# A differential-attention encoder on one core: the heads' norm factors sent through DRAM instead of through TensorE, and a branch's splits spread over four merge tiles

## The chip, the core and the metric

The kernel runs on one core of a Trainium2 chip. A core has TensorE (PE; its weight loads are listed as PEld), VectorE (DVE), ScalarE (ACT), GpSimd (POOL), and SyncE (SP), whose queue issues nearly all DMAs of this kernel. On-chip tensors lie on 128 partitions; TensorE writes to accumulation banks of 128 x 512 floats, of which there are eight. The time is that of the device in microseconds (us); the profile is of one further execution of the same program.

## The reference, cut to what matters

Two sequences of 512 tokens go through one encoder layer. Three branches (a state-space branch, a differential attention, an attention to a memory) are computed from the normed input, each is projected up, gated and added, and an output projection and a gated feed-forward layer follow. The change lies in the differential attention's norm and in the merge of the branches:

```python
def _diff_attention(q, k, v, lam, subln_g, lambda_init):
    ...
        w = probs[:, :, 0] - lam * probs[:, :, 1]
        return jnp.einsum('bhqk,bkhe->bqhe', w.astype(v.dtype), v)
    ...
    o = _rmsnorm(o, subln_g) * (1.0 - lambda_init)
    return o.reshape(Bn, L, DIFF_WIDTH)

def _layer(x, mem, l, p):
    ...
    branches = (y_s5, y_diff, y_x)
    merged = None
    for n in range(N_BRANCH):
        term = jax.nn.sigmoid(g[..., n * D_MODEL:(n + 1) * D_MODEL]) * (branches[n] @ p['w_up'][l, n])
        merged = term if merged is None else merged + term
    x = x + merged @ p['w_out'][l]
```

There are 4 differential heads of width 128, `D_MODEL` is 1024 and a branch is 512 wide. The norm is over the 128 features of one head, one factor for each token.

## The kernel before

Activations lie transposed: features on partitions, tokens along the free dimension. A float32 product is made of three products of rounded parts: each operand is split into a high and a low part (`split`: ScalarE makes the high part, VectorE the low one), and `mm3` adds high x high, high x low and low x high into one bank, 512 columns at a time. A weight tile is loaded to `wf` (two buffers), split to `wh` and `wl` (two buffers each), and used.

The stage of the change is the differential attention. Its 32 steps run over 4 heads, 2 sequences and 4 blocks of 128 queries (`steps`, (h, s, qt)). Step i goes through the loop at the end in stages, one turn of the loop apart:

- `score` makes two maps' scores in banks of the pool `sc` (three banks) and the softmax parts on VectorE and ScalarE: `nb` is the negated maximum, `e` the exponentials, later the weighted difference of both maps, `r` the reciprocal sums.
- `turn` transposes `e` on TensorE (bank `bktr`, two banks) and splits it to `pH` and `pL`.
- `outputs` multiplies with the values for each pair of blocks, into the one bank `oo`; after the fourth block ScalarE copies it to `osb` (features x tokens).
- `squares`, after the fourth block, transposes `osb`, sums squares on ScalarE into `ss` (tokens on partitions), and adds the softmax's part of epsilon.
- `normed`, one turn later, makes the factors and scales. `factor` first calls `root`: a square root on ScalarE and a reciprocal on VectorE, `rs`, 128 x 4: one factor for each token, tokens on partitions. To scale `osb`, whose tokens lie along the free dimension, the factors have to stand on all partitions along that dimension; `spread` does this by four transposes of a broadcast column each into a bank. VectorE scales `osb` from that bank, and SP stores it to `bD[1, h]` in DRAM.

All of this is laid between other products. `queue` is a list of generators (projections of the next heads, gates, the merges), and `fill(10)`, called twice in each turn, takes about ten products from it. TensorE's order is the program's order from here on (`PE.on`). The order on the other engines and on SP's queue is set by a scheduler when the program is built: an instruction may stand well ahead of its place in the code.

The last generator is `merges`. For the output tiles m = 0 to 7 it multiplies the first branch (n = 0) with `w_up[0, m]` into two banks of the pool `mm`, which has two banks in all; VectorE takes each out with its gate, `mg <- gl, bkmm`. Then the third branch (n = 2) follows in the same way, `gl <- gl, bkmm`, with a sum on GpSimd. A branch comes back from DRAM by `merge_part`: a load of 128 x 1024 from `bD[n, t]` into `yt` (one of the four buffers `ld`, which gates and gate loads use too) and a split to `yh` and `yl`. Before the change `merge_in(2)` makes all four parts of the third branch at tile m = 5 of the first. After the attention loop the second branch (n = 1, the differential one) is split between the last products of the queue and merged last.

`mbc` is a tile of 128 x 512 that an earlier stage uses for the memory's norm factors and nobody after that.

Of the kernel before, what the change touches and what calls it, by code (L numbers as in the profile page):

```python
# [10 lines left out]
F32 = mybir.dt.float32  # L11
# [3 lines left out]
ALU = mybir.AluOpType  # L15
# [4 lines left out]
P = 128  # L20
L = 512
DM = 1024
KD = DM // P
NS = 2
# [46 lines left out]
def encoder(ctx: ExitStack, tc: tile.TileContext, a, out, out_t):  # L71
    nc = tc.nc
    V, S, PO, PE, SP = (InOrder(tc, e_) for e_ in (nc.vector, nc.scalar, nc.gpsimd, nc.tensor, nc.sync))
# [17 lines left out]
    def open_tags(es, side=None, **tags):  # L91

        for tag, n in tags.items():
            pools[tag] = es.enter_context(tc.tile_pool(name=tag, bufs=n, side=side, reuse_waits="tile"))
# [12 lines left out]
    drp = ctx.enter_context(tc.tile_pool(name="drp", bufs=1, space=DRAM))  # L107

    def slot(tag, shape=(P, NT), dt=F32, name="sl"):
        return pools[tag].tile(list(shape), dt, tag=tag, name=name)  # L110
# [21 lines left out]
    def split(hi, lo, src, scale=None):  # L132

        if scale is None:
            h = S.copy(hi, src)
            l_ = V.tensor_tensor(out=lo, in0=src, in1=hi.bitcast(F32), op=ALU.subtract)
        else:
            h = S.activation(out=hi, in_=src, func=AF.Copy, scale=scale)
            l_ = V.scalar_tensor_tensor(out=lo, in0=src, scalar=scale, in1=hi.bitcast(F32), op0=ALU.mult, op1=ALU.subtract)
        return h, l_  # L140
# [64 lines left out]
    def root(ss, n, nt=4, bias=epsc):  # L205

        rs = rp.tile([P, 4], F32, tag="rs", name="rs", bufs=4)
        S.activation(out=rs[:, :nt], in_=ss[:, :nt], func=AF.Sqrt, scale=1.0 / n, bias=bias)
        V.reciprocal(rs[:, :nt], rs[:, :nt])
        return rs  # L210

    def factor(ss, n, nt=4, bias=epsc):
        rs = root(ss, n, nt, bias)
        return rs, spread(rs, nt)

    def spread(rs, nt=4):

        bc = aux()
        for t in range(nt):
            PE.transpose(bc[:, t * P : (t + 1) * P], rs[:, t : t + 1].broadcast_to([P, P]), ident)  # L220
        return bc
# [24 lines left out]
    def sums(src, tag="wb", ss=None, ts=range(4)):  # L246

        if ss is None:
            ss = rp.tile([P, 4], F32, tag="ss", name="ss", bufs=3)
        for t in ts:  # L250
            tk = slot(tag, [P, DM], name="tk")
            SP.dma_start(tk, src[t])
            S.activation(out=tk, in_=tk, func=AF.Square, accum_out=ss[:, t : t + 1])
        return ss
# [107 lines left out]
    bc = spread(rs)  # L362
# [26 lines left out]
    bc = spread(rs)  # L389
# [102 lines left out]
    g04 = cst.tile([P, 1], F32, name="g04")  # L492
# [81 lines left out]
    with behind():  # L574

        mrs = cst.tile([P, 4], F32, name="mrs")
        mbc = cst.tile([P, L], F32, name="mbc")
        rs_, bc = factor(sums(a["memN"], "ld"), DM)
# [65 lines left out]
    def fill(n):  # L644
        nonlocal owed
        owed += n
        while owed > 0 and queue:
            r = next(queue[0], None)
            if r is None:
                queue.pop(0)  # L650
            else:
                owed -= r
        if not queue:
            owed = 0
# [5 lines left out]
    def units(src, hi, lo, use, nk=KD):  # L660

        wh, wl = weight(src, nk * P)
        for s in range(NS):
            cs = slice(s * L, (s + 1) * L)
            o = bank()
            for k in range(nk):
                mm3([o], wh, wl, [(hi[k][:, cs], lo[k][:, cs])], k, nk)
                if k == nk - 1:
                    use(s, o)
                if k % 2 == 1:  # L670
                    yield 6

    def gate_units():
        t = next(todo)
        gt = slot("ld", name="gt")

        def use(s, o):
            S.activation(out=gt[:, s * L : (s + 1) * L], in_=o, func=AF.Tanh, scale=0.5)

        yield from units(a["w_in"][20 + t], xh, xl, use)  # L680
        SP.dma_start(gD[t], gt)
# [43 lines left out]
    steps = [(h, s, lt) for h in range(4) for s in range(NS) for lt in range(4)]  # L725
# [3 lines left out]
    for i in range(-AHEAD, len(steps) + 1):  # L729
        if i + AHEAD < len(steps):  # L730
            h, s, lt = steps[i + AHEAD]
# [18 lines left out]
        if 0 <= i < len(steps):  # L750
            h, s, lt = steps[i]
# [8 lines left out]
        if i > 0 and steps[i - 1][2] == 3:  # L760
            h, s, _ = steps[i - 1]
# [7 lines left out]
            osb = xa.tile([P, L], F32, tag="osb", name="xosb", bufs=1)  # L769
# [57 lines left out]
    def merge_part(n, t, tag="y"):  # L827
        h_, l_ = (slot(tag, [P, NT], F32R, f"y{c}{t}") for c in "hl")
        yt = slot("ld", name="yt")
        SP.dma_start(yt, bD[n, t])  # L830
        split(h_, l_, yt, scale=(0.125, None, 0.5)[n])
        return h_, l_

    def merge_in(n, tags="yyyy"):
        return list(zip(*(merge_part(n, t, tags[t]) for t in range(4))))

    def merge_units(n, b, m, first=False, last=False):
        gt = slot("ld", name="gl")
        SP.dma_start(gt, gD[n * KD + m])
        if first:  # L840
            mg[m] = slot("mg", name=f"mg{m}")

        def use(s, o):
            cs = slice(s * L, (s + 1) * L)
            dst = mg[m] if first else gt
            V.scalar_tensor_tensor(out=dst[:, cs], in0=gt[:, cs], scalar=1.0, in1=o, op0=ALU.add, op1=ALU.mult)

        yield from units(a["w_up"][n, m], *b, use, 4)
        if not first:
            PO.tensor_tensor(out=mg[m], in0=mg[m], in1=gt, op=ALU.add)  # L850
        if last:
            mgh[m] = slot("ms", [P, NT], F32R, f"mgh{m}")
            mgl[m] = slot("ms", [P, NT], F32R, f"mgl{m}")
            split(mgh[m], mgl[m], mg[m])
# [4 lines left out]
    def first_in(t):  # L859
        parts0[t] = merge_part(0, t, ("qk", "qk", "qk", "v")[t])  # L860
        if len(parts0) == 4:
            b0.append(list(zip(*(parts0[t_] for t_ in range(4)))))

    def merges():
        res_.close()
        xp_es.close()
        open_tags(mes, side="right", mg=8, y=8)
        for m in range(KD):
            if m == 5:
                b2 = merge_in(2)  # L870
            yield from merge_units(0, b0[0], m, first=True)
        for m in range(KD):
            yield from merge_units(2, b2, m)

# [7 lines left out]
    for _ in gate_units():  # L882
# [3 lines left out]
    queue += [qk_units(1, True), dk[1], gate_units(), qk_units(2, True), dk[2], v1_, qk_units(3, True), dk[3], gate_units(),  # L886
              gate_units(), merges()]
    s0, ss, osb = {}, {}, {}

    def score(i):  # L890
        nonlocal last_e
        h, s, qt = steps[i]
        cs = slice(s * L, (s + 1) * L)
        if h and s == qt == 0:
            finish(dk[h])
        if qt == 0:
            s0[h, s] = acol.tile([P, 4], F32, tag="s0", name="s0", bufs=3)
        q_, k_, er = qk[h, True], qk[h, False], []
        qs_ = slice(s * L + qt * P, s * L + (qt + 1) * P)
        sc = [bank("sc") for _ in MAPS]  # L900
        for mp in range(2):
            PE.matmul(sc[mp], q_[mp][:, qs_], k_[mp][:, cs], start=True, stop=False)
            PE.matmul(sc[mp], q_[mp][:, qs_], k_[2 + mp][:, cs], start=False, stop=True)
        for mp in range(2):
            er.append(softmax_parts(ap_, acol, sc[mp], L, 1.0, f"d{mp}", None if mp else s0[h, s][:, qt : qt + 1]))
        (e0, sm0), (e1, r1) = er
        V.scalar_tensor_tensor(out=r1, in0=r1, scalar=nlam, in1=sm0, op0=ALU.mult, op1=ALU.mult)
        last_e = last_x, V.scalar_tensor_tensor(out=e0, in0=e1, scalar=r1, in1=e0, op0=ALU.mult, op1=ALU.add)
        es[i] = e0
# [32 lines left out]
    def squares(i):  # L942
# [9 lines left out]
        V.scalar_tensor_tensor(out=s0[h, s], in0=s0[h, s], scalar=EPS * P, in1=s0[h, s], op0=ALU.mult, op1=ALU.mult)  # L952
        V.tensor_tensor(out=ss[h, s], in0=ss[h, s], in1=s0[h, s], op=ALU.add)

    def normed(i):
        h, s, _ = steps[i]
        _, bc = factor(ss[h, s], P, bias=0.0)
        V.scalar_tensor_tensor(out=osb[h, s], in0=osb[h, s], scalar=g04, in1=bc, op0=ALU.mult, op1=ALU.mult)
        SP.dma_start(bD[1, h, :, s * L : (s + 1) * L], osb[h, s])

    n = len(steps)
    for i in range(-1, n + 3):
        if i + 1 < n:
            score(i + 1)
        if i in (22, 23):
            first_in(2 * i - 44)
        fill(10)
        if i in (21, 22):
            first_in(3 if i == 21 else 1)
        if 0 <= i < n:  # L970
            turn(i)
        if 0 < i <= n and steps[i - 1][2] % 2:
            outputs(i - 1)
        fill(10)
        if 1 < i <= n + 1 and steps[i - 2][2] == 3:
            squares(i - 2)
        if i > 2 and steps[i - 3][2] == 3:
            normed(i - 3)
    aes.close()
    phase.close()  # L980
    ves.close()
# [334 lines left out]
    for i in range(1, KFF - 1):  # L1316
        n = i + 1
# [209 lines left out]
    for v, (m, lo_, hi_) in enumerate(VISITS):  # L1527
# [24 lines left out]
        if v == 0:  # L1552
# [3 lines left out]
            y = [y2[m // 2][:, m % 2] for m in range(KD)]  # L1556
# [40 lines left out]
    for i, (c0, n) in enumerate(parts):  # L1597
        before, acc = acc if i else None, new_acc()
        for m in range(KD):
# [7 lines left out]
            if i and m == 3:  # L1607
                bc = spread(rs)
# [30 lines left out]
    bc = spread(rs, 3)  # L1639
# [461 lines left out]
```

## Time and profile before

| | us |
|---|---|
| three runs: median (lowest to highest) | 1585.29 (1582.87 to 1586.84) |
| the profiled execution, its own time | 1587.09 |
| its span, from the first instruction to the last | 1584.2 |
| differential attention with the merges laid into it | about 535 to 762 |
| first to last transposes of norm factors there | 572.7 to 759.6 |
| stores of scaled heads, `bD<-osb`, first to last issue | 574.1 to 760.9 |

In the lists a row of a timeline is start, duration, engine, line, operation, written tile <- read tiles, shapes, and in brackets how long the engine stood idle before it and who released it. All compute instructions pass through one helper and carry its line, L62, so that tiles tell them apart. A list of DMAs gives the number of issues, the size of one and the median time from issue to landing. A list by stage gives busy time of each engine, the granted TensorE clock, the share of time in which the DMA engines were busy, and GB/s.

### The profile page before, as it was taken

What the parts mean: (1) busy time and instruction counts of PE and PEld (TensorE: products, weight loads), DVE (VectorE), ACT (ScalarE), POOL (GpSimd) and SP (SyncE); (2) the same over time, 40 slices, a digit from 0 to 9 for tenths busy, and PEclk for the clock granted to TensorE, in tenths of its full rate; (3) what the DMA queues carried; (4) which work ended last, traced back from release to release, by engine and by line L of the source; (5) the groups of instructions that cost most, each with busy time, mean ns of one, the idle gap of its engine ahead of it and who ended that gap; (6) DMA issues with size and microseconds to landing.
All of it is one profiled execution on the core that took longest, in us unless ns stands there. A gap on an engine that the chain in (4) does not pass through costs nothing.

```text
span 1584.2 us, 21534 instructions
## 1 busy us (share of the span) xinstructions
PE 1573.7 (99%) x7701; PEld 1320.9 (83%) x7701; DVE 1119.0 (71%) x1777; ACT 627.2 (40%) x1112; POOL 510.5 (32%) x406
## 2 busy tenths in 40 slices
PE   9999999999999999999999999999999999999998
PEld 7888888888898889888888888888888888878887
DVE  5897688665766676866445567777767777999664
ACT  7354322346553356564223353232333223333222
POOL 0001000001432221300343335767655542445353
PEclk9999999999999999999999999999999999999999
DMA  9643362567655543354544433555433241786632
GB/s 350 208 144 142 102 222 80 184 192 257 205 180 163 149 117 84 110 186 167 175 156 154 153 100 126 179 183 182 160 126 133 107 153 69 272 279 202 212 120 106
DMA packets 118970, 261.04 MB, mean 165 GB/s; under 512 B 15824, under 2 KB 51920, under 8 KB 118864
## 3 DMA queue, kind: packets, MB, share of 16 engines
q1 hardware_dynamic: 117856, 256.80, 48.6%
q10 hardware_dynamic: 1008, 2.88, 0.5%
q8 instruction: 60, 0.98, 0.2%
q14 instruction: 46, 0.38, 0.1%
HBM read 172.89 MB, written 74.15 MB: 156 GB/s over the span
## 4 chain that ended last, share of the span: by engine, by line
PE 94%; DVE 2%; DMA 2%; ACT 1%; issue 1%; SPq 0%; DVEq 0%; ACTq 0%
PE bkmm L62 81%; PE bktr L62 8%; PE bksc L62 3%; PE bkoo L62 2%; DVE tl L62 1%; DMA tk<-in_memN 1%; DMA acc<-in_w_fo 0%; DMA wf<-in_w_mv 0%; DVE ts L62 0%; DVE y L62 0%; ACT tk L62 0%; DVE u L62 0%; ACT th L62 0%; DVE w L62 0%; ACT L62 0%
## 5 line engine op out<-in xcount | busy, mean ns | idle before, releaser
L62 PE MATMUL bkmm<-xh,wh 128*128 128x512 f32 x640 | 252.7, 395 | 0.0
L62 PE MATMUL bkmm<-xl,wh 128*128 128x512 f32 x640 | 250.7, 392 | 0.0
L62 PE MATMUL bkmm<-xh,wl 128*128 128x512 f32 x640 | 249.8, 391 | 0.0
L62 PE MATMUL bkmm<-th,whl 128*128 128x512 f32 x696 | 227.3, 390 | 0.0
L62 ACT CAST wh<-wf 128x1024 fp32r<-128x1024 f32 (+1 forms) x131 | 116.1, 886 | 228.1 <-PE bkmm L62 189.2
L62 DVE TENSOR_TENSOR wl<-wf,wh 128x1024 fp32r<-128x1024 f32 (+1 forms) x132 | 141.5, 1072 | 69.3 <-ACT wh L62 66.0
L62 PEld LDWEIGHTS bkmm<-th,whl 128*128 128x128 f32 x696 | 130.6, 188 | 27.2 <-issue 0.2
L62 PEld LDWEIGHTS bkmm<-xh,wl 128*128 128x128 f32 x640 | 120.2, 188 | 25.5 <-issue 0.2
L62 PE MATMUL bkmm<-th,w 128*128 128x512 f32 x432 | 140.4, 391 | 0.9 <-DVE up L62 0.5
L62 POOL TENSOR_TENSOR raw<-raw 128x128 f32<-128x128 f32 x144 | 90.5, 629 | 155.7 <-DMA raw<-in_w_fo 128.9
L62 PEld LDWEIGHTS bkmm<-xh,wh 128*128 128x128 f32 x640 | 120.3, 188 | 23.3 <-issue 0.2
L62 PEld LDWEIGHTS bkmm<-xl,wh 128*128 128x128 f32 x640 | 120.4, 188 | 23.1 <-issue 0.6
L62 PE MATMUL bkmm<-tl,whl 128*128 128x512 f32 x348 | 135.4, 389 | 0.0
L62 POOL TENSOR_TENSOR ws<-wf 128x512 f32<-128x512 f32 x44 | 70.3, 1598 | 148.3 <-DMA wf<-in_w_fu 139.6
L62 DVE TENSOR_TENSOR whl<-ws,whl 128x1024 fp32r<-128x1024 f32 x44 | 78.7, 1788 | 55.1 <-ACT whl L62 55.1
L62 PE MATMUL bkmm<-th,wh 128*128 128x512 f32 x260 | 101.3, 390 | 0.0
L62 PE MATMUL bkmm<-th,wl 128*128 128x512 f32 x260 | 101.2, 389 | 0.0
L62 PE MATMUL bkmm<-tl,wh 128*128 128x512 f32 x260 | 101.2, 389 | 0.0
L62 PEld LDWEIGHTS bkmm<-th,w 128*128 128x128 f32 x432 | 81.1, 188 | 20.2 <-DVE u L62 1.6
L62 POOL TENSOR_TENSOR mg<-mg,gl 128x1024 f32<-128x1024 f32 x16 | 44.2, 2763 | 136.4 <-DMA bD<-osb 94.1
L62 PE MATMUL bkmm<-tl,w 128*128 128x512 f32 x216 | 84.1, 389 | 0.0
L62 ACT ACTIVATE e<-bksc,nb 128x512 f32<-128x512 f32 (+1 forms) x96 | 58.9, 616 | 60.8 <-DVE nb L62 60.3
(644 smaller groups left out, 3598.6 us busy)
## 6 DMA issues: line engine op xcount, KB each, us to landing
wf<-in_w_in SPq DMA_DIRECT2D x40, 512.0 KB, 4.1
wD<-hl SPq DMA_DIRECT2D x36, 512.0 KB, 2.9
w<-wD SPq DMA_DIRECT2D x36, 512.0 KB, 3.6
gD<-gt SPq DMA_DIRECT2D x24, 512.0 KB, 2.9
gl<-gD SPq DMA_DIRECT2D x24, 512.0 KB, 3.3
raw<-in_w_fo SPq DMA_DIRECT2D x88, 128.0 KB, 3.4
wf<-in_w_fg SPq DMA_DIRECT2D x22, 512.0 KB, 4.0
wf<-in_w_fu SPq DMA_DIRECT2D x22, 512.0 KB, 3.5
```

Source lines behind the costliest of these rows:

```text
L62: ins = do(*args, **kw)
```

## The change

The eight calls of `factor` in `normed` go. In their place three stages follow `squares`: `rooted` makes the factors and stores them, element by element, to a row of `rD` in DRAM, in the order of the tokens; `spread_in`, two turns later, loads that row of 512 onto all 128 partitions of `mbc`; `normed`, one turn after that, scales from `mbc`. The loop runs three turns longer. In `merges`, the four parts of the third branch are made one at a time, ahead of the first branch's tiles 2 to 5. The number of those splits stays.

```diff
@@ merges
+        b2 = []
         for m in range(KD):
-            if m == 5:
-                b2 = merge_in(2)
+            if 2 <= m < 6:
+                b2.append(merge_part(2, m - 2, "y"))
             yield from merge_units(0, b0[0], m, first=True)
+        b2 = list(zip(*b2))
         for m in range(KD):
             yield from merge_units(2, b2, m)
@@ the attention
+    rD = drp.tile([4 * NS, 4, P], F32, name="rD")
@@
+    def rooted(i):
+        h, s, _ = steps[i]
+        SP.dma_start(rD[NS * h + s].rearrange("t p -> p t"), root(ss[h, s], P, bias=0.0))
+
+    def spread_in(i):
+        h, s, _ = steps[i]
+        SP.dma_start(mbc, rD[NS * h + s].rearrange("t p -> (t p)").unsqueeze(0).broadcast_to([P, L]))
+
     def normed(i):
         h, s, _ = steps[i]
-        _, bc = factor(ss[h, s], P, bias=0.0)
-        V.scalar_tensor_tensor(out=osb[h, s], in0=osb[h, s], scalar=g04, in1=bc, op0=ALU.mult, op1=ALU.mult)
+        V.scalar_tensor_tensor(out=osb[h, s], in0=osb[h, s], scalar=g04, in1=mbc, op0=ALU.mult, op1=ALU.mult)
         SP.dma_start(bD[1, h, :, s * L : (s + 1) * L], osb[h, s])
 
     n = len(steps)
-    for i in range(-1, n + 3):
+    for i in range(-1, n + 6):
@@
-        if i > 2 and steps[i - 3][2] == 3:
-            normed(i - 3)
+        for d, do in ((3, rooted), (5, spread_in), (6, normed)):
+            if d <= i < n + d and steps[i - d][2] == 3:
+                do(i - d)
```

TensorE's order loses the eight groups of four transposes and is otherwise the same. On the other engines the scheduler sets a new order. VectorE's rows at the seventh of the eight factors (head 3, first sequence), before; `rs` is the factors' reciprocal, `mg` the emptying of a merge bank, `wl` and `yl` the low parts of a weight and of a branch, `pL` that of a turned block:

```order
L62 TENSOR_SCALAR yl_7726<-yt,yh_7725 128x1024
L62 TENSOR_TENSOR pL<-bktr,pH 128x4x128
L62 RECIPROCAL r<-sm 128x1
L62 RECIPROCAL rs<-rs 128x4
L62 TENSOR_SCALAR r<-r,nlam,s_7423 128x1
L62 TENSOR_SCALAR mg_7640<-gl,bkmm 128x512
L62 TENSOR_SCALAR e<-e,r 128x512
L62 TENSOR_SCALAR s_7423<-s_7423 128x4
L62 TENSOR_SCALAR osb<-osb,g_3098,bktr 128x512
L62 TENSOR_SCALAR mg_7640<-gl,bkmm 128x512
L62 TENSOR_TENSOR wl<-wf,wh 128x512
```

The scaling of `osb` stands between the two emptyings of one merge tile, `mg_7640`. The same place on VectorE in the changed kernel, where that tile is `mg_7641`:

```order
L62 TENSOR_TENSOR ss<-ss,s_7112 128x4
L62 RECIPROCAL r<-sm 128x1
L62 RECIPROCAL rs<-rs 128x4
L62 TENSOR_SCALAR r<-r,nlam,s_7403 128x1
L62 TENSOR_SCALAR e<-e,r 128x512
L62 TENSOR_SCALAR s_7403<-s_7403 128x4
L62 TENSOR_TENSOR pL<-bktr,pH 128x4x128
L62 TENSOR_SCALAR mg_7641<-gl,bkmm 128x512
L62 TENSOR_SCALAR osb<-osb,g_3098,mbc 128x512
L62 TENSOR_SCALAR mg_7641<-gl,bkmm 128x512
L62 TENSOR_TENSOR wl<-wf,wh 128x512
```

The scaling, now from `mbc`, still stands between the two emptyings; the first of them has moved behind `e` and `pL`, and the split `yl` of the third branch no longer stands here. On SP's queue, the rows at the same factor in the changed kernel:

```order
L62 DMA wf<-in_w_up 128x512
L62 DMA rD<-rs 128x4x1
L62 DMA mbc<-rD 128x512
L62 DMA bD<-osb 128x512
L62 DMA gl<-gD 128x1024
L62 DMA wf<-in_w_up 128x512
```

Store, load and the scaled head's store follow one another directly, with a gate's load and a weight's load behind them. VectorE's rows at the first factor (head 0, first sequence) in the changed kernel:

```order
L62 RECIPROCAL rs<-rs 128x4
L62 TENSOR_SCALAR r<-r,nlam,s_5593 128x1
L62 TENSOR_SCALAR e<-e,r 128x512
L62 TENSOR_SCALAR s_5593<-s_5593 128x4
L62 TENSOR_REDUCE nb<-bksc 128x1 x2
L62 TENSOR_SCALAR osb<-osb,g_3098,mbc 128x512
L62 TENSOR_TENSOR t_5888<-bkmm,rc 128x512
L62 STREAM_SHUFFLE t_5890<-bkmm 128x512
L62 RECIPROCAL r<-sm 128x1
L62 TENSOR_SCALAR r<-r,nlam,s_5862 128x1
L62 TENSOR_SCALAR e<-e,r 128x512
```

Before the change the scaling stood ahead of the two `nb` rows; the rest of this place is as it was.

## The prediction

> **What bounds the kernel now.** I read the page's busy times first, then its chain of waits, then the list of who waits for whom on TensorE, then the stage in which the change lies.
>
> ```profile
> PE 1573.7 (99%) x7701; PEld 1320.9 (83%) x7701; DVE 1119.0 (71%) x1777; ACT 627.2 (40%) x1112; POOL 510.5 (32%) x406
> ...
> PE 94%; DVE 2%; DMA 2%; ACT 1%; issue 1%; SPq 0%; DVEq 0%; ACTq 0%
> ...
> PE bkmm L62 <- ACT wh L62: 1.1, 1, 1.1
> ...
> PE bktr L62 <- DVE rs L62: 0.8, 1, 0.8
> ...
> 560.00:762.00 202.00, 202.00 (x1145) 174.79 (x1144) 141.55 (x267) 114.93 (x267) 24.73 (x16) 1.00 0.44 134
> ```
>
> TensorE is busy 99% of the span and is 94% of the chain that ends last; its longest single wait for another engine is 1.1 us. From 560 to 762 us, where all eight norm factors are made and spread, it has no idle time, at a granted clock of 1.00. So here an instruction taken from TensorE is worth what it holds TensorE, and a new wait costs only when it runs past the slack that other engines have against TensorE's fixed order. Of 202 us, VectorE uses 142, ScalarE 115, and the DMA engines are 44% busy: room, but in lumps.
>
> **What is removed: 32 transposes on TensorE.** A busy TensorE is not TensorE at its peak, so I price a group by the starts around it.
>
> ```profile
> L62 PE MATMUL bktr<-ident,rs x32: 270/272/287, 572.7 to 759.6; 128*128 128x128 f32 x32
> ...
> 572.50 0.39 PE L62 MATMUL bkmm<-xh,wl 128*128 128x512 f32 x1
> 572.73 0.60 PE L62 MATMUL bktr<-ident,rs 128*128 128x128 f32 x4
> 573.08 0.48 PE L62 MATMUL bksc<-h,q 128*128 128x512 f32 x1
> 573.40 0.39 PE L62 MATMUL bksc<-l,q 128*128 128x512 f32 x1
> 573.63 0.40 PE L62 MATMUL bksc<-h,q 128*128 128x512 f32 x1
> ```
>
> Ordinary 512-column products start 0.23 us apart (572.50 to 572.73, 573.40 to 573.63). From the start of the four transposes to the second product after them it is 573.40 - 572.73 = 0.67; without them it would be 0.23. A group costs 0.44 us, and eight cost 8 x 0.44 = 3.5 us. The Trainium skill (TensorE: Matmul & The Clock Gate, Part 4: PE-mode transpose) gives a transpose about 275 ns in one kernel's context. The row's duration, 272 ns, agrees, but durations overlap here: the four take 0.60 together. By durations the sum would be another, and that is a rival below.
>
> **What is added: a round trip through DRAM for each head and sequence.** The factors (128 x 4, 2 KB) are stored to `rD` element by element, read back as one row of 512 onto all 128 partitions (256 KB), and VectorE's scaling of `osb` takes `mbc` instead of a bank. That is 16 more DMA issues on SP, none on POOL. Neither transfer stands in the trace; the nearest rows are
>
> ```profile
> gD<-gk SPq DMA_DIRECT2D x16, 2.0 KB, 1.7
> ...
> zy<-yD SPq DMA_DIRECT2D x32, 64.0 KB, 3.9
> ...
> bD<-osb SPq DMA_DIRECT2D x8, 256.0 KB, 2.0
> ...
> q<-hl SPq DMA_DIRECT2D x32, 128.0 KB, 2.3
> ...
> wf<-in_w_up SPq DMA_DIRECT2D x24, 256.0 KB, 3.0
> ...
> yt<-bD SPq DMA_DIRECT2D x12, 512.0 KB, 3.4
> ```
>
> For the store, 1.7 us below (the same 2 KB in fewer pieces) and 3.9 above (the slowest of the finely cut ones); I take 2.0, since it is nearest in size to the first and `bD<-osb` from the same place lands in that. For the load, 2.3 below and 3.4 above; I take 3.0, the row of 256 KB from DRAM. With 0.3 allowed for two hand-overs between queues (an allowance, no row), the time c from the reciprocal's end to the factors on all partitions is 5.3 us, between 4.0 and 7.3. The Trainium skill (DMA: Bandwidth & Descriptors, Rules for kernel authors) says that a non-contiguous last dimension becomes one descriptor per element, here an estimated 512; it speaks against this store, no row shows one, and it is the ground of the slow rival.
>
> The load waits on SP for the store, and `osb` on VectorE for the load. What is queued behind them there is read from the rows of the new order shown with the change. Although the code places the scaling three steps later, at the seventh factor (head 3, first sequence) VectorE still has it six instructions behind the reciprocal `rs`, and ahead of the second `mg<-gl,bkmm`, which empties a bank of the merges, and of a weight's split `wl`. A split of the third branch that stood ahead of the reciprocal is gone. The times of that place:
>
> ```profile
> 733.01 1.08 ACT L62 ACTIVATE yh<-yt 128x1024 fp32r<-128x1024 f32 x1
> ...
> 735.02 1.22 DVE L62 SCALAR_TENSOR_TENSOR yl<-yt,yh 128x1024 fp32r<-128x1024 f32 x1
> ...
> 737.95 0.18 DVE L62 RECIPROCAL rs<-rs 128x4 f32<-128x4 f32 x1 [1.05 <-ACT rs L62]
> ...
> 739.49 0.74 DVE L62 SCALAR_TENSOR_TENSOR osb<-osb,g,bktr 128x512 f32<-128x512 f32 x1
> ...
> 740.75 0.69 DVE L62 SCALAR_TENSOR_TENSOR mg<-gl,bkmm 128x512 f32<-128x512 f32 x1 [0.52 <-PE bkmm L62]
> ...
> 746.68 0.69 DVE L62 SCALAR_TENSOR_TENSOR mg<-gl,bkmm 128x512 f32<-128x512 f32 x1 [2.05 <-PE bkmm L62]
> ```
>
> The `mm` pool has two banks. The bank emptied at 740.75 is the one that VectorE waits for at 746.68; its 12 products take 2.72 us (the distance of the emptyings at 762.70 and 765.42, quoted next), 0.227 each. So TensorE needs it at 746.68 - 2.72 = 743.96, or 743.5 once the 0.44 is gone. The emptying now ends at 738.13 + c + 0.74 + 0.69, so TensorE stalls for c - 3.9. The third branch's splits, moved to tiles 2 to 5, take 1.08 us of ScalarE and 1.22 of VectorE from ahead of this reciprocal; if it comes 1.2 earlier, the limit is 5.2.
>
> The eighth factor, in the same pure merges, and the first, in the attention steps:
>
> ```profile
> 757.38 0.17 DVE L62 RECIPROCAL rs<-rs 128x4 f32<-128x4 f32 x1
> ...
> 762.70 0.69 DVE L62 SCALAR_TENSOR_TENSOR gl<-gl,bkmm 128x512 f32<-128x512 f32 x1 [1.24 <-PE bkmm L62]
> ...
> 765.42 0.69 DVE L62 SCALAR_TENSOR_TENSOR gl<-gl,bkmm 128x512 f32<-128x512 f32 x1 [0.54 <-PE bkmm L62]
> ...
> 571.57 0.18 DVE L62 RECIPROCAL rs<-rs 128x4 f32<-128x4 f32 x1 [1.35 <-ACT rs L62]
> ...
> 575.66 0.69 DVE L62 TENSOR_TENSOR t<-bkmm,rc 128x512 f32<-128x512 f32 x1 [0.35 <-PE bkmm L62]
> ...
> 577.34 1.68 DVE L62 SCALAR_TENSOR_TENSOR e<-e,r 128x512 f32<-128x512 f32 x1
> ...
> 582.31 0.60 PE L62 MATMUL bktr<-ident,e 128*128 128x128 f32 x4
> ```
>
> At the eighth, the first emptying of the third branch comes behind `osb`: 757.55 + c + 1.43 must be by 762.70 + 2.72 - 0.44 = 764.98, so c may be 6.0. At the first, `osb` stood ahead of both `nb` and now stands behind them, with the next step's `t`, shuffle, `r` and `e` queued after it. The softmax's `e` now ends c + 0.74 + 3.36 (575.66 to 579.02) after 571.75, and TensorE turns it at 582.31 - 0.44: again c up to 6.0. In the other five I found no earlier limit and give them nothing.
>
> **SP.** While SP waits for the store, weights and gates queue behind. The widest such hold is at the seventh, where the `wf` load that SP issued at 742.07 stands behind `mbc` and `bD<-osb`:
>
> ```profile
> 742.07 0.33 SPq L62 DMA_DIRECT2D wf<-in_w_up  x1
> ...
> 753.35 0.62 ACT L62 CAST wh<-wf 128x512 fp32r<-128x512 f32 x1 [4.65 <-PE bkmm L62]
> ```
>
> Its buffer is cast two weights later, at 753.35, and that cast waits for TensorE and not for the load: 742.07 + 3.0 leaves 8 us. I cost this at nothing; with the cover gone it would cost what c exceeds about 13. **The rest.** The splits keep their number and size, and spread out they only share four `ld` buffers with the gates' loads for longer; the loop's three further turns issue 60 products that would have followed anyway, so the second branch's splits move behind part of the third branch, of which the last three tiles (3 x 24 products of 0.227, 16 us) still lie between them and their use, against 1.08 + 1.22 us for a split. Nothing for both; their cover gone would show as a wait for `yh` at the start of the second branch.
>
> **The sum.** Gain 3.5. The cost, by the three limits, is (c - 5.2) + (c - 6.0) + (c - 6.0), each only where positive: 0.1 us at 5.3; I take 0.5, since c varies from one to the next. Net -3.0 us. For the profiled execution 1587.09 - 3.0 = 1584.1 (its span 1584.2 to 1581.2, with the same 2.9 around it). It stands 1.8 above the median of the runs, 1585.29, which becomes 1582.3.
>
> **The rivals.** *The round trip is slow, and it ends slower than before* (chance 0.20). One mechanism: VectorE, in its order, stands at `osb` until `mbc` lands, and the two merge banks behind it stay full. The gain is eaten where (c - 5.2) + 2(c - 6.0) = 3.5, at c = 6.9; with both DMA bounds at their upper rows, c = 7.3, the stalls are 2.1 + 1.3 + 1.3 = 4.7 and the time is 1586.5, or 1587.8 if the moved splits bring nothing and the seventh's limit stays 3.9. At c = 8.5 it is 0.3% slower. For it: an order that puts the scaling close behind the reciprocal, and a store cut finer than any in the trace. Against it: 2 KB in 1.7 us. *The transposes are worth their durations* (0.07): 32 x 0.272 = 8.7 us, 1576.6. This is where the skill's 275 ns per transpose, charged singly, would lead. Against it stand the starts 0.35 apart for four. *The gain is absorbed* (0.08): TensorE arrives earlier and waits for `e` or `wl` instead, 1585.3. For it, VectorE, on which the softmax steps run, is busy 142 of 202 us; against it, TensorE has no idle time in this stage that such a pacing would leave.
>
> **How the numbers follow.** The forecast has 0.65. The runs before lie 2 us to either side of their median, and 0.3% (4.8 us) is about what a measurement of this kernel can tell from no change. The forecast's -3.0 is inside that; I put a quarter of its chance, 0.15, past it. Faster: 0.15 + 0.07 = 0.22. Slower: of the slow rival's 0.20 some 0.12, for c of 8.5 and more: past the quoted rows, but a store of 5.2 instead of 2.0 suffices, and no row has one cut this fine. Within: 0.66. The range goes from the gain in full with the runs' 2 us (1585.29 - 3.5 - 2.0 = 1579.8) to the slow rival at its upper rows, 1587.8.
>
> **What would show it.** Right: TensorE's count down by 32, no new idle time between 560 and 800, landings of `rD<-rs` near 2.0 and `mbc<-rD` near 3.0, and VectorE's waits for `mbc` short. Wrong on c: a store landing over 4 us, with VectorE's `osb` waiting for DMA and TensorE for VectorE's `mg` or `gl`. Wrong on the splits: the seventh reciprocal no earlier against its `mg`. Wrong on SP: a `wh` that waits for `wf`.

## The result, and the profile after

The changed kernel is 4.3% slower: 1654.96 us (median of 5 runs, 1651.43 to 1656.04) against 1585.07 us for the kernel before beside it (5 runs, 1582.87 to 1586.84), ratio 1.0433, 95% interval 1.0423 to 1.0444. The forecast was 1582.3 us, its range ended at 1587.8. The profiled execution took 1655.86 us, its span 1654.0 us, which is 69.8 us more than before.

The page of the changed kernel: busy times, the granted clock in 40 slices, and the chain of waits by engine and by line.

```profile
PE 1590.3 (96%) x7669; PEld 1332.6 (81%) x7669; DVE 1119.6 (68%) x1777; ACT 626.0 (38%) x1112; POOL 511.2 (31%) x406
...
PEclk9999999999999998998889999999999999999999
...
PE 81%; DMA 10%; DVE 4%; ACT 3%; issue 2%; SPq 1%; POOL 1%; DVEq 0%; ACTq 0%; POOLq 0%
PE bkmm L62 71%; PE bktr L62 6%; DMA rD<-rs 4%; DMA mbc<-rD 2%; PE bkoo L62 1%; PE bksc L62 1%; DMA acc<-in_w_fo 1%; SPq L62 1%; POOL t L62 1%; ACT L62 1%; DMA tk<-in_xN 1%; ACT e L62 1%; DMA tk<-in_memN 1%; DVE nb L62 1%; DMA xt<-in_xT 0%
```

The 32 transposes are gone (7701 less 7669). Two transfers that did not exist before now make up 6% of the chain that ends last, and TensorE's part of it fell from 94% to 81%. Next, the landings of the two new transfers; what VectorE waited for from 560 to 840 us; and what TensorE waited for from 540 to 900 us (total, times, longest):

```profile
mbc<-rD SPq DMA_DIRECT2D x8, 256.0 KB, 4.9
...
rD<-rs SPq DMA_DIRECT2D x8, 2.0 KB, 8.7
```

```profile
DVE osb L62 <- DMA mbc<-rD: 72.9, 8, 11.1
```

```profile
PE bktr L62 <- DVE e L62: 19.0, 3, 6.6
PE bkmm L62 <- DVE mg L62: 15.5, 2, 7.7
PE bkmm L62 <- DVE wl L62: 8.7, 2, 7.6
PE bkmm L62 <- DVE gl L62: 7.8, 1, 7.8
PE bkoo L62 <- DVE pL L62: 3.5, 1, 3.5
```

The store lands 8.7 us after its issue, where I had priced 2.0; the load 4.9, where I had 3.0. VectorE stands at the scaling for 9 us on average at every one of the eight factors, and TensorE then waits for whatever VectorE has behind it. One such place, the seventh factor, as a timeline of VectorE, SP and TensorE:

```profile
786.28 0.18 DVE L62 RECIPROCAL rs<-rs 128x4 f32<-128x4 f32 x1 [1.35 <-ACT rs L62]
...
786.49 0.37 SPq L62 DMA_DIRECT2D rD<-rs  x1
...
787.94 0.68 DVE L62 SCALAR_TENSOR_TENSOR mg<-gl,bkmm 128x512 f32<-128x512 f32 x1
794.51 0.32 SPq L62 DMA_DIRECT2D mbc<-rD  x1
799.59 0.75 DVE L62 SCALAR_TENSOR_TENSOR osb<-osb,g,mbc 128x512 f32<-128x512 f32 x1 [10.97 <-DMA mbc<-rD]
800.26 0.68 DVE L62 SCALAR_TENSOR_TENSOR mg<-gl,bkmm 128x512 f32<-128x512 f32 x1
...
800.99 0.79 PE L62 MATMUL bkmm<-yh,wh 128*128 128x512 f32 x1 [7.75 <-DVE mg L62]
```

The factors' reciprocal ends at 786.46 and the scaling starts at 799.59: c, the time from the reciprocal's end to the factors on all partitions, is 13.1 us, not 5.3. The second emptying of the merge tile follows at once, and the product that needs its bank has stood for 7.75 us.

The stage from 540 to 900 us, before and then after (busy times of TensorE, its weight loads, VectorE, ScalarE and GpSimd, granted clock, share of busy DMA engines, GB/s):

```profile
540.00:900.00 360.00, 360.00 (x1859) 306.12 (x1858) 230.08 (x387) 165.38 (x337) 85.29 (x43) 1.00 0.46 144
```

```profile
540.00:900.00 360.00, 305.32 (x1513) 258.27 (x1512) 190.01 (x339) 136.21 (x304) 63.98 (x32) 0.91 0.42 119
```

TensorE had no idle time there and now has 360 - 305.3 = 54.7 us, which is the sum of the waits above to 0.2. The granted clock is 0.91 instead of 1.00. What that means is seen in TensorE's starts around a pause (the sixth factor):

```profile
758.47 0.39 PE L62 MATMUL bkmm<-yl,wh 128*128 128x512 f32 x1
758.69 0.39 PE L62 MATMUL bkmm<-yh,wl 128*128 128x512 f32 x1
766.82 0.79 PE L62 MATMUL bkmm<-yh,wh 128*128 128x512 f32 x1 [7.74 <-DVE mg L62]
767.41 0.63 PE L62 MATMUL bkmm<-yl,wh 128*128 128x512 f32 x1
767.84 0.63 PE L62 MATMUL bkmm<-yh,wl 128*128 128x512 f32 x1
768.26 0.63 PE L62 MATMUL bkmm<-yh,wh 128*128 128x512 f32 x1
```

Before the pause the products start 0.22 us apart, after it 0.43. So the 69.8 us are 54.7 of pauses, less the 3.5 that the transposes were forecast to bring, and by difference 69.8 - 54.7 + 3.5 = 18.6 of slower pace after the pauses. The Trainium skill (TensorE: Matmul & The Clock Gate, Part 1: The HAM clock gate) says that after an idle window of about 3.4 us the clock is halved until the engine has been busy for about as long. The trace agrees on the half: its record of the granted clock falls to 0.50 at each of the eight longest pauses (3.5 to 7.8 us) and returns 2.9 to 6.0 us after the pause has ended, which is up to nearly twice the page's time. TensorE is busy for 38.3 us of the stage at that clock; half of that, 19.2 us, is close to the 18.6 found by difference.

### The profile page after: what moved, and what is told of

It is laid out like the page before. It is cut to its first block, busy times and chain, and to the rows that moved or that the text cites. A ratio compares the mean times of both kernels' runs of the same rounds, so it can differ in the third digit from the quotient of the medians.

```text
span 1654.0 us, 21492 instructions
## 1 busy us (share of the span) xinstructions
PE 1590.3 (96%) x7669; PEld 1332.6 (81%) x7669; DVE 1119.6 (68%) x1777; ACT 626.0 (38%) x1112; POOL 511.2 (31%) x406
## 4 chain that ended last, share of the span: by engine, by line
PE 81%; DMA 10%; DVE 4%; ACT 3%; issue 2%; SPq 1%; POOL 1%; DVEq 0%; ACTq 0%; POOLq 0%
PE bkmm L62 71%; PE bktr L62 6%; DMA rD<-rs 4%; DMA mbc<-rD 2%; PE bkoo L62 1%; PE bksc L62 1%; DMA acc<-in_w_fo 1%; SPq L62 1%; POOL t L62 1%; ACT L62 1%; DMA tk<-in_xN 1%; ACT e L62 1%; DMA tk<-in_memN 1%; DVE nb L62 1%; DMA xt<-in_xT 0%
## 5 line engine op out<-in xcount | busy, mean ns | idle before, releaser
L62 PE MATMUL bkmm<-yh,wh 128*128 128x512 f32 x192 | 78.2, 408 | 23.3 <-DVE mg L62 15.5
L62 PEld LDWEIGHTS bkmm<-th,w 128*128 128x128 f32 x432 | 81.1, 188 | 19.2 <-DVE up L62 1.8
```

What stands on the lines that cost most here:

```text
L62: ins = do(*args, **kw)
```

## The experiments

Times are medians; each ratio is to the kernel before, run beside it on the same chip.

**1. The splits alone.** The kernel before with the change's other part:

```diff
-            if m == 5:
-                b2 = merge_in(2)
+            if 2 <= m < 6:
+                b2.append(merge_part(2, m - 2, "y"))
```

> The kernel before with one part of the change alone: the third branch's splits spread over four merge tiles; the norm factors still go by transposes. Theory (the stalls come from the scaling that stands on VectorE and waits for the factors' round trip): without a round trip there is nothing to wait for, 1584 to 1587 us, granted clock 1.00. Rival (the moved splits share in the loss, since they fill VectorE ahead of the factors): 10 us or more slower than before, and TensorE's pauses of several us between 640 and 760 stay.

1585.73 us, ratio 1.0000 (0.9990 to 1.0009). The splits alone change nothing that can be measured.

**2. The round trip alone.** The changed kernel with the reverse of that diff.

> The changed kernel with the third branch's splits put back at one tile: the round trip through DRAM alone. Theory: the round trip carries the whole loss, about 1655 us, with eight pauses of TensorE of 5 to 9 us and c (reciprocal's end to factors on all partitions) near 13 us; by my limit of 3.9 instead of 5.2 at the seventh factor it may be 1 to 2 us longer than the changed kernel. Rival (the splits' new place costs part): 1640 us or less.

1661.6 us, ratio 1.0477 (1.0461 to 1.0492). The round trip carries the whole loss and more: this kernel takes 6.6 us more than the changed one (1661.6 - 1655.0). The surplus can't be credited to the splits. TensorE's pauses in the stage are 60.0 us instead of 54.7, and 3.5 of these 5.3 us lie at the first four factors, where every engine's order is still the same in both kernels; c is 13.8 to 15.3 us there, against 12.7 to 14.0. At the seventh, where my two limits, 3.9 and 5.2, foresaw 1.3 us more, TensorE waited no longer (7.3 us against 7.75). Why the round trip took longer in this run stays open.

**3. VectorE's order alone.** The scaling is held back until the emptying and the step's `e` that the code names before it have been issued; the scheduler then puts it 11 to 34 instructions behind its reciprocal.

```diff
-        V.scalar_tensor_tensor(out=osb[h, s], in0=osb[h, s], scalar=g04, in1=mbc, op0=ALU.mult, op1=ALU.mult)
+        with ExitStack() as held:
+            for ins in (last_e[1], last_v):
+                if ins is not None:
+                    held.enter_context(tc.issue_after(ins.ins))
+            V.scalar_tensor_tensor(out=osb[h, s], in0=osb[h, s], scalar=g04, in1=mbc, op0=ALU.mult, op1=ALU.mult)
```

> The changed kernel, with only VectorE's order changed: each scaling of osb stands behind the attention steps' e and the merges' emptyings that the code names before it, 9 to 34 rows behind its reciprocal. Store, load and SP's order of them are as in the changed kernel. Theory (a slow round trip costs time only since VectorE stands waiting for it): store still lands in 7 to 10 us and load in 4 to 5, but TensorE's long pauses are gone, the granted clock is 1.00 again, and the time is 1580 to 1588 us, near the forecast's 1582. Rival A (SP's queue, held by the load that waits for the store, starves weights and gates): pauses of TensorE stay and name wl, wh or a DMA, 1600 us or more. Rival B (the transfers themselves slow the chip): the granted clock stays under 0.95 between 560 and 850 us.

1604.03 us, ratio 1.0120 (1.0102 to 1.0138). 51 of the 69 us go although the store lands as late as ever. But 18 us stay, more than the theory allowed. The profiled execution, at 1598.8 us, is the shortest of the four. Its landing of the store, the stage, TensorE's longest wait, and what SP waited for from 660 to 800 us:

```profile
rD<-rs SPq DMA_DIRECT2D x8, 2.0 KB, 8.9
```

```profile
540.00:900.00 360.00, 347.03 (x1762) 292.51 (x1761) 223.60 (x375) 158.26 (x330) 81.74 (x41) 0.99 0.51 144
```

```profile
PE bksc L62 <- ACT e L62: 8.7, 3, 6.1
```

```profile
SPq L62 <- DMA rD<-rs: 39.1, 5, 8.6
```

The wait of 6.1 us is for a softmax's `e` on ScalarE. The rows of SP and ScalarE ahead of it:

```profile
713.42 0.73 SPq L62 DMA_DIRECT2D rD<-rs  x1
...
721.84 0.32 SPq L62 DMA_DIRECT2D mbc<-rD  x1
722.30 0.34 SPq L62 DMA_DIRECT2D yt<-bD  x1
...
728.39 1.06 ACT L62 ACTIVATE yh<-yt 128x1024 fp32r<-128x1024 f32 x1 [9.14 <-DMA yt<-bD]
```

ScalarE had itself stood 9.14 us for a branch's load, and that load stood on SP behind the one that waits for the store, from 713.4 to 721.8. Rival A describes this place: the wait has moved from VectorE to the transfers behind.

**4. The store in 128 pieces of 16 bytes** instead of 512 of 4; the factors then lie in another order of the tokens, so the scaled heads carry factors of other tokens.

```diff
-        SP.dma_start(rD[NS * h + s].rearrange("t p -> p t"), root(ss[h, s], P, bias=0.0))
+        SP.dma_start(rD[NS * h + s].rearrange("t p -> (t p)").rearrange("(p t) -> p t", t=4), root(ss[h, s], P, bias=0.0))
```

> The changed kernel with each factor store written as 128 pieces of 16 contiguous bytes instead of 512 pieces of 4 bytes; the factors therefore land in another order of the tokens, and the scaled heads carry factors of other tokens. Load and VectorE's order are as they were. Theory P (the store's landing goes by its number of pieces, or by pieces that share a line): it lands in 2 to 4 us instead of 8.7, c is 7 to 8.5 us, and by the three limits the stalls are (c - 5.2) + 2 (c - 6.0) = 4 to 8 us and as much again at the other five factors: 1588 to 1605 us. Rival (a small store followed by a load of it takes this long whatever its pieces): it still lands in about 8 us, c stays near 13, about 1655 us.

1592.39 us, ratio 1.0040 (1.0024 to 1.0056): 62.6 us less than the changed kernel, with VectorE's wait left in its place.

```profile
mbc<-rD SPq DMA_DIRECT2D x8, 256.0 KB, 4.2
...
rD<-rs SPq DMA_DIRECT2D x8, 2.0 KB, 1.4
```

So a small store into DRAM that is read back at once is not slow in itself; the one of the changed kernel was slow by its form. That form has two sides, the number of pieces and where they lie.

**5, 6, 10, 11. The same 512 pieces, further apart.** The store keeps its 512 pieces of 4 bytes, each on W numbers of its own (W = 16, 128, 4, 2: 64, 512, 16, 8 bytes). The load reads one contiguous row that overlaps the stored pieces and was filled once beforehand, so the scaling takes other values than the factors.

```diff
-    rD = drp.tile([4 * NS, 4, P], F32, name="rD")
+    rD = drp.tile([4 * NS, 4 * P, W], F32, name="rD")
+    SP.dma_start(rD.rearrange("k n w -> k (n w)")[:, :L], mbc[: 4 * NS, :])
...
-        SP.dma_start(rD[NS * h + s].rearrange("t p -> p t"), root(ss[h, s], P, bias=0.0))
+        SP.dma_start(rD[NS * h + s, :, 0].rearrange("(t p) -> p t", p=P), root(ss[h, s], P, bias=0.0))
...
-        SP.dma_start(mbc, rD[NS * h + s].rearrange("t p -> (t p)").unsqueeze(0).broadcast_to([P, L]))
+        SP.dma_start(mbc, rD[NS * h + s].rearrange("n w -> (n w)")[:L].unsqueeze(0).broadcast_to([P, L]))
```

> The changed kernel, with each of the 512 four-byte pieces of a factor store on a line of 64 bytes of its own (in the changed kernel 16 pieces from 16 partitions lie on one such line). The load still reads one contiguous row of 2 KB that overlaps the stored pieces, so it waits for the store as before but brings other numbers: the scaling takes values that are not the factors. Theory S (pieces on the same line are written one after the other): the store lands in 2 to 4 us and the time is 1588 to 1605 us. Theory N (the landing goes by the number of pieces): it lands in 7 to 10 us, 1645 to 1665 us.

> As the run before, but each four-byte piece on 512 bytes of its own. Theory S with a line of 64 bytes: as the run before, 2 to 4 us and 1588 to 1605 us. Theory S with a line longer than 64 bytes: this one lands in 2 to 4 us though the run before did not. Theory N: both land in 7 to 10 us, 1645 to 1665 us.

> The changed kernel with the 512 four-byte pieces of a store 16 bytes apart, so that 4 instead of 16 lie on a line of 64 bytes; the load brings other numbers, as in the runs with 64 and 512 bytes. Theory S in proportion (each further piece on a line adds the same): (8.7 - 2.0) / 15 = 0.45 us for each, the store lands in 2.0 + 3 x 0.45 = 3.3 us, c is near 7 and the time about 1590 to 1600 us. Rival (all or nothing: any sharing of a line costs the whole): 7 us or more and 1640 us or more.

> As the run with 16 bytes, with the pieces 8 bytes apart, 8 on a line of 64 bytes. Theory S in proportion: 2.0 + 7 x 0.45 = 5.1 us, c near 9, and by the three limits (c - 5.2) + 2 (c - 6.0) = 10 us and as much again at the other five factors: 1600 to 1615 us. Rival (all or nothing): 7 us or more and 1640 us or more.

The store's row in the lists of DMAs of these four, at 64, 512, 16 and 8 bytes in this order:

```profile
rD<-rs SPq DMA_DIRECT2D x8, 2.0 KB, 2.0
```

```profile
rD<-rs SPq DMA_DIRECT2D x8, 2.0 KB, 1.9
```

```profile
rD<-rs SPq DMA_DIRECT2D x8, 2.0 KB, 2.9
```

```profile
rD<-rs SPq DMA_DIRECT2D x8, 2.0 KB, 4.8
```

| distance of the 4-byte pieces (pieces within 64 bytes) | store lands, us | time, us | ratio |
|---|---|---|---|
| 4 bytes (16), the changed kernel | 8.7 | 1654.96 | 1.0433 (1.0423 to 1.0444) |
| 8 bytes (8) | 4.8 | 1608.99 | 1.0143 (1.0126 to 1.0160) |
| 16 bytes (4) | 2.9 | 1594.44 | 1.0054 (1.0039 to 1.0069) |
| 64 bytes (1) | 2.0 | 1589.06 | 1.0022 (1.0013 to 1.0031) |
| 512 bytes (1) | 1.9 | 1589.35 | 1.0022 (1.0011 to 1.0033) |

The count of pieces is the same in all five rows, and so is the time in which they are moved: by the trace's DMA packets, the first store of each of these kernels has moved all its pieces 1.3 us after its issue, while it lands after 7.8, 4.4, 3.1, 2.3 and 1.9 us. In the changed kernel that store is issued at 570.8 us and lands at 578.6, and from 572.2 to 578.5 no packet moves at all. So what grows is the time behind the packets, and it follows how close the pieces lie. Theory N falls, and so does the rival that any sharing costs the whole. Theory S in proportion forecast 3.3 and 5.1 us, and 2.9 and 4.8 were measured.

The size of the line is not settled. A distance of 64 bytes is enough (512 buy nothing over it), 16 is not, and 32 was not run. Counted on lines of 64 bytes, each further piece adds 0.3 us from 1 to 4 pieces, 0.48 from 4 to 8 and 0.49 from 8 to 16. Counted on lines of 32 bytes, where the same rows have 1, 2, 4 and 8 pieces, it adds 0.9, 0.95 and 0.98, which is the more even. That pieces on one line are written one after the other remains a reading of these times; no view shows the writing itself. Why four pieces of 16 bytes within 64 land in 1.4 us and four of 4 bytes in 2.9 stays open too, since their number and size changed together.

**7. Both remedies, the whole computation.** Runs 3 and 4 together, with the scaling undoing the order of the pieces:

```diff
-            V.scalar_tensor_tensor(out=osb[h, s], in0=osb[h, s], scalar=g04, in1=mbc, op0=ALU.mult, op1=ALU.mult)
+            o4 = osb[h, s].rearrange("q (t p) -> q t p", t=4)
+            V.scalar_tensor_tensor(out=o4, in0=o4, scalar=g04, in1=mbc.rearrange("q (p t) -> q t p", t=4), op0=ALU.mult, op1=ALU.mult)
```

> The changed kernel with both remedies: the store in 128 pieces of 16 bytes, whose order the scaling undoes by reading mbc with a stride of four, and the scaling late in VectorE's order. The whole computation is done. Theory: with the store at 1.4 us SP is held for only 2 us a time and nothing stands behind the scaling, so the pauses are gone and the removed transposes show: before minus 3.5 us and up to 1 us back, 1582 to 1584 us, ratio 0.998 to 0.999. Rival (the gain of the transposes is absorbed by other waits of VectorE and SP): 1585 to 1590 us.

1583.25 us (11 runs, 1582.15 to 1585.12) against 1585.70 (26 runs), ratio 0.9988 (0.9979 to 0.9997): faster than both kernels, and than the one before by 2.4 us. Its stage and all of TensorE's waits in it:

```profile
540.00:900.00 360.00, 358.95 (x1834) 304.34 (x1833) 234.44 (x386) 164.74 (x338) 87.33 (x43) 1.00 0.50 150
```

```profile
PE bkmm L62 <- ACT wh L62: 0.6, 1, 0.6
PE bktr L62 <- DVE e L62: 0.5, 1, 0.5
```

3.5 from the transposes less 1.05 of pauses is 2.45, near the 2.4 measured (the interval of the ratio allows 0.5 to 3.3).

**8 and 9. Who is held by the slow store.** Run 3 with the load issued by GpSimd (8), then with the store issued by GpSimd too (9).

```diff
-        SP.dma_start(mbc, rD[NS * h + s].rearrange("t p -> (t p)").unsqueeze(0).broadcast_to([P, L]))
+        PO.dma_start(mbc, rD[NS * h + s].rearrange("t p -> (t p)").unsqueeze(0).broadcast_to([P, L]))
```

> The run with the late scaling and the store in 4-byte pieces, with the load of mbc issued by GpSimd instead of SP, so that GpSimd and not SP stands waiting for the store. Theory (what is left of the loss there, 18 us, is SP held by the load, which makes the branch's and weights' loads behind it late): the pauses of 6.3 us at 726 and of 3.0 us at 785 go, the store still lands in about 9 us, and the time is 1582 to 1590 us. Rival (the 18 us come from the late scaling itself or from the DMA engines): 1598 us or more.

> As the run with the late scaling and the load issued by GpSimd, with the store in 4-byte pieces issued by GpSimd as well, so that nothing that SP issues stands behind it in its queue. Theory Q (transfers issued behind the slow store in the same queue land after it, as in the traces so far, where they landed 0.2 to 2.0 us after the store): SP's loads land in their usual 2 to 5 us next to a store that still takes 7 to 11, and the time falls from 1605 to 1582 to 1592 us. Rival (the slow store holds the DMA engines for every queue): SP's loads still land late beside it and the time stays at 1600 us or more.

1605.20 us, ratio 1.0128 (1.0114 to 1.0141), and 1606.40 us, ratio 1.0126 (1.0106 to 1.0147). Both theories fall, and both times are those that the rivals forecast: neither freeing SP nor taking the store out of SP's queue brings the 18 us back. Run 8's rival named the late scaling itself or the DMA engines; run 7 has the same late scaling and loses nothing, which speaks for the DMA engines. In run 9, the rows of the store at the seventh factor, of two loads that SP issued 2.4 and 3.0 us after it on its own queue, and of the work that waited for the second:

```profile
750.91 0.76 POOL L62 DMA_DIRECT2D rD<-rs  x1 [21.27 <-DVE r L62]
...
753.33 0.32 SPq L62 DMA_DIRECT2D gl<-gD  x1
753.93 0.33 SPq L62 DMA_DIRECT2D wf<-in_w_up  x1
...
765.34 0.62 ACT L62 CAST wh<-wf 128x512 fp32r<-128x512 f32 x1 [4.78 <-DMA wf<-in_w_up]
```

That `wf`, asked for by itself, landed 11.3 us after its issue:

```profile
DMA to landing us min/median/max: 11.3/11.3/11.3
```

Its median in the same run is 3.3. The store had landed 9.7 us after 750.91, at 760.6; the load of 753.93, from another queue, came 4.7 us behind it. The closest case is at the second factor, where a copy `h<-hl` that touches neither `rD` nor `rs` was issued by SP at 601.02 and landed after 8.6 us, at 609.6 (median 2.4 in this run), beside a store of GpSimd's issued at 600.59 that landed after 8.8, at 609.4:

```profile
DMA to landing us min/median/max: 8.6/8.6/8.6
```

The copy of the same kind that SP issued at 600.5, just ahead of that store, landed in 2.3 us. In the whole of run 9 the trace has the landings of 24 transfers that were issued between a slow store's issue and its landing, and none of them landed before the store. So the slow store holds back the landing of what is issued after it, also from another engine's queue. The Trainium skill (DMA: Bandwidth & Descriptors, Queues, rings and completion order) states a rule that fits: the write that tells of a transfer's end waits for all earlier writes of the same DMA engine, across its queues. The row of the copy agrees. At the seventh factor more is held than the telling: from 753.3 to 756.5 us the DMA engines move nothing (share 0.00, 0 GB/s), though the first load stands issued from 753.3 and the second from 753.9. What holds the packets themselves stays open.

GpSimd's own work stood behind its waits in runs 8 and 9, which may add to them; how much was not measured apart.

## Why the prediction was wrong

**The step that failed first is the price of the store.** I took 2.0 us, by 2 KB that landed in 1.7 in the row `gD<-gk`, and 3.9 as the upper bound, from rows of larger transfers. None of these rows says how the pieces lie: by its packets, a transfer of that row is 32 pieces of 64 bytes. Here 512 pieces of 4 bytes lie next to one another, 16 within each 64 bytes, and the store lands in 8.7 us. With the load at 4.9 (priced 3.0) c became 12.7 to 14.9 instead of 5.3. The number of pieces, of which I had warned, was the wrong suspect: 512 pieces that lie 64 bytes apart land in the 2.0 us that I took. (My bounds of c, 4.0 and 7.3, also leave out the 0.3 that the 5.3 contains; nothing hangs on it at 13.)

**The three limits were right.** Rows of the first and the eighth factor, reciprocal and scaling:

```profile
570.57 0.18 DVE L62 RECIPROCAL rs<-rs 128x4 f32<-128x4 f32 x1 [1.35 <-ACT rs L62]
...
583.43 0.75 DVE L62 SCALAR_TENSOR_TENSOR osb<-osb,g,mbc 128x512 f32<-128x512 f32 x1 [9.77 <-DMA mbc<-rD]
...
817.49 0.17 DVE L62 RECIPROCAL rs<-rs 128x4 f32<-128x4 f32 x1
...
831.35 0.75 DVE L62 SCALAR_TENSOR_TENSOR osb<-osb,g,mbc 128x512 f32<-128x512 f32 x1 [10.43 <-DMA mbc<-rD]
```

c is 12.7 at the first and 13.7 at the eighth. My formula gives 12.7 - 6.0 = 6.7 and 13.7 - 6.0 = 7.7; the waits for `e` and `gl` there are 6.6 and 7.8. At the seventh 13.1 - 5.2 = 7.9, against 7.75. At these three places the mechanism and the limits of the slow rival stood; only c was off.

**"In the other five I found no earlier limit and give them nothing"** is the second step that failed. The three account for 6.6 + 7.75 + 7.8 = 22.2 of the 54.7 us; the other 32.5 lie at the factors in between, where TensorE waited for `e`, `wl`, `mg` and `pL`, all but 1.3 of it for work that stood behind the scaling on VectorE. I had looked at three places and carried no limit for the rest. This counts even at my own price. In run 5 the store lands in 2.0 us and the load in 3.6, and at my three places c is 5.4, 5.4 and 5.9, as priced; at the other five it is 5.3 to 9.6. The kernel is not 3.0 us faster but 3.4 slower (ratio 1.0022), with these waits in the stage:

```profile
PE bkmm L62 <- DVE wl L62: 2.4, 1, 2.4
PE bksc L62 <- ACT e L62: 0.8, 1, 0.8
PE bktr L62 <- DVE e L62: 0.5, 1, 0.5
PE bkmm L62 <- DVE mg L62: 0.3, 1, 0.3
```

By the starts of its products (each distance less the usual one of that product, summed from 540 to 900 us) TensorE loses 8.8 us there and lost 1.5 before: 7.3 more, less 3.5, is 3.8 and near the 3.4 measured. The longest wait, for `wl`, is at the second factor, and it ends at 605.9 us, ahead of that factor's own scaling, whose load is issued only at 605.4. So it is not a wait behind that scaling: VectorE comes late to `wl`. That it does so because it stood 2.5 us for `mbc` at the first factor is argued, not shown; with the late order of run 7, where it doesn't stand there, the wait is gone.

**The pace after a pause** was in no term: some 18.6 us here. With single pauses of at most 2.4 us the stage's mean granted clock stays at 1.00 (runs 4, 5 and 10), with a longest pause of 3.3 it is 0.98 (run 11), with 7.8 it is 0.91. The length alone does not decide it: in run 5 the clock is 0.50 from 607.3 to 610.7 us, after the pause of 2.4, while a pause of the same length at the same place left it at 1.00 in runs 4 and 10.

**SP "at nothing"** failed in kind, not in the changed kernel's sum. I followed the weights behind the load and found 8 us of cover; the branch's load `yt<-bD` has none, and the hold is not SP's alone but of everything issued after the store. While VectorE stood for longer, this was hidden; run 3 laid it open, 18 us.

**The gain of the transposes** stood: with the round trip out of the way 2.4 us were measured (interval of the ratio: 0.5 to 3.3 us), against 3.5 by the starts and 8.7 by durations. **The splits** cost nothing alone, as said.

Of the signs named, those against c came as written: a store over 4 us, `osb` waiting for DMA, TensorE for `mg` and `gl`.

## What to carry to other kernels

Before a bounce through DRAM is priced by its bytes, look at how its pieces lie: 2 KB that many partitions wrote in neighbouring pieces of 4 bytes took 8.7 us to land here, the same pieces 64 bytes apart 2.0, and one contiguous run for each partition (with the reader undoing the order) 1.4. Ask of every engine what stands behind the instruction that waits, at all places where it occurs and not at the three that come to mind; a scaling that nobody needs soon belongs late in the queue. And a slow transfer is also a delay for those issued after it, from other queues too.

## What the runs showed that I had not expected

- A 2 KB store of 512 pieces of 4 bytes lands in 1.9 us or in 8.7, by the distance of the pieces alone, though the pieces have been moved after 1.3 us in both cases.
- A copy that has nothing to do with the store, issued on another queue 0.4 us after it, landed in 8.6 us; the one issued 0.1 us before the store landed in 2.3.
- After pauses of 7 us TensorE's products start 0.43 us apart instead of 0.22; that added about a third to the loss of the pauses themselves (18.6 to 54.7).
